# Summing fewer feature tiles of the second weight chunk in the startup of a two-layer mixer

## The chip, the core and the metric

The kernel runs on one core of a Trainium2 chip, as one program. The metric is device time in microseconds. The time before is 1073.24 us, the median of three runs (1071.56 to 1074.11). The profile is one execution, with a time of each instruction on the engines: PE multiplies matrices, DVE (VectorE) and ACT (ScalarE) work on tiles, SP issues the DMAs. "PE row" below means one matmul with 512 columns.

## The reference, cut

```python
# two layers; x (256 latent tokens x 2048), ctx (256 context tokens x 2048)
shift, scale, gate = split(silu(c) @ ada_w[l] + ada_b[l], 3)          # and the same for c_ctx
h  = rmsnorm(x, norm_g[l]) * (1 + scale) + shift                      # and hc from ctx
q, k, v, up, uf, g = split_proj(h @ w_in[l])
att = latent_attention(rope(rmsnorm(q)), [kc; rope(rmsnorm(k))], [vc; v])
mixed = concat(att, multiscale_pool(up), fourier_mix(uf))
x = x + gate * ((mixed * silu(g)) @ w_out[l])
...
return rmsnorm(x, final_norm_g)
```

What matters for this change is the first line of layer 0: the modulation needs 33.5 MB of `ada_w` before `h` is whole, and the products of `h` can begin feature tile by feature tile.

## The kernel before

Everything is kept transposed in 16 feature tiles of 128; latent and context tokens stand side by side (T = 512). Each product of float32 operands is made of three matmuls (high x high, high x low, low x high: `mm3`). `split` makes the two halves of a tile: ACT casts the high half (L138), DVE subtracts to get the low half (L139). Weights come as `raw` by DMA (L145) and are split to `whi` and `wlo`; each of the three names has three buffers. SP issues all loads in one queue, in an order that the scheduler sets; a load that waits for its buffer holds those behind it.

**The startup** of layer 0 (`startup`) makes `h0` and begins its products while the modulation loads.

- The statistics: the squares of x (ACT L862, DVE L860, sums L868), a product with ones (PE L871), then `rstd` (ACT L878, DVE L880). `load_x` brings x in four parts of 1 MB; three are asked for at once, the fourth behind the first piece of the modulation.
- The modulation comes in ten groups of 1 or 2 feature tiles (`GROUPS`: group 0 is tile 0, group 1 tile 1, group 2 tiles 2 and 3, ... group 7 tiles 12 and 13, group 8 tile 14, group 9 tile 15), each of four pieces (`a`, DMA L976, four buffers). `ada_part` multiplies a piece (PE L981). From group 5 on one piece of the four is done on DVE instead (`dvec`, L965).
- When a group's last piece is done, ACT copies the sums (`ev`, L1018), PE turns them (L1024), DVE reduces them (`red`, L1031) and adds the bias (L1038 to L1040), and `make_h` makes the group's tiles of `h`: DVE multiplies (L248, L255), ACT casts (L138), DVE subtracts (L139). The next group's sums use the same PSUM buffer and so wait for `red`.
- PE's order is written out by hand. `queue` puts a group's products on a list, ready one or two steps later, and `work(n)` issues n of them (L932) between the modulation's matmuls: 14 behind a piece of a group of two tiles, 7 behind one of a single tile, and 4 on either side of the turning.

The products of the startup are the first chunk of `w_in` (`accs`, 4 PSUM accumulators), the second chunk (`first`, 4 accumulators) and six tiles of the gate, three (`gfirst`) over the first `KG` = 4 feature tiles and three (`early`) over all. Eight PSUM buffers hold four large sums (`mm`) and four others (`sm`), so `accs` can only begin when `first` has been copied to `part` in SBUF. Before, `first` sums `KS` = 8 feature tiles; then chunk 0 is made up over tiles 0 to 7, and from tile 8 on it goes along with the modulation. Behind the startup `b_chunk` sums the second chunk's other tiles (L335 to L337), two tiles to a piece of weights, and adds `part`. `FILL` sets how many units of layer 1's modulation (DVE L188) each piece brings along.

`warm` issues matmuls of ones with ones, whose result is not used. `LAG_E` is the number of microseconds of queued products that PE puts between the evacuation of a chunk and the first use of it, for q the transposes at L525.

Of the kernel before, what the change touches and what calls it, by code (L numbers as in the profile page):

```python
# [12 lines left out]
F32 = mybir.dt.float32  # L13
# [7 lines left out]
P = 128  # L21
# [4 lines left out]
T = N + C  # L26
# [3 lines left out]

AHEAD = 400
ST = 4
KS = 8
ND = (0, 0, 0, 0, 0, 1, 1, 1, 1, 1)
KG = 4
NE = 3
# [10 lines left out]
LAG_S, LAG_T, LAG_E, LAG_Q = 4.3, 1.4, 5.6, 0.0  # L47
# [1 line left out]
LOW = -400  # L49
CHAIN = 200  # L50
PRE = 6
FILL = ((1.69, 1.5, 0.55, 1.43, 1.0), (0.04, 1.61, 0.01, 0.66, 0))
VB, VG, VF, VS, VC, VW = 0, 96, 128, 144, 152, 184


# [1 line left out]
def backbone(  # L57
# [24 lines left out]
    V, S, G, PE = nc.vector, nc.scalar, nc.gpsimd, nc.tensor  # L82

    const = ctx.enter_context(tc.tile_pool(name="const", bufs=1))
    hp = ctx.enter_context(tc.tile_pool(name="hp", bufs=1))
# [28 lines left out]
    def load_x(g, n):  # L114
        for j in range(0, 4, n):
            nc.sync.dma_start(xk[g][:, j : j + n], xT[:, 4 * g + j : 4 * g + j + n])
# [167 lines left out]
    side = Side()  # L284
# [86 lines left out]
    def f4(s, shape, dt=F32R):  # L371
        return late["f4"].tile(list(shape), dt, tag="f4", name=name(s))
# [145 lines left out]
    def q_prep(qraw, qT, rq):  # L518
        rq.append(head_rstd(qraw, 4, P ** -0.5))
        for tt, r in qraw:  # L520
            qo = rope_one(tt, r, 4, 0)
            yield 0.0, 3.0 if tt == 0 else 1.0
            tp = smt()
            for hh in range(4):
                PE.transpose(tp[:, hh * P : hh * P + P], qo[:, hh], idt)  # L525
            c = slice(tt * P, tt * P + P)
            split(tp.rearrange("p (h n) -> p h n", h=4), qT[0][:, :, c], qT[1][:, :, c])
            yield 0.43, 0.0
# [47 lines left out]
    def layer(l, h, xs, chunk0):  # L576
# [62 lines left out]
        for g in range(2):  # L639
            accs = b_chunk(l, 3 + g, h, ntt, FILL[l][2])  # L640
            qraw = evac_raw(accs)
            if l == 0:
                side.finish("a0")
                qT = pair8(4, (T,))
            else:
                qT = [a.rearrange("p a (b n) -> p (a b) n", b=2) for a in pair8(2, (2 * N,))]
            rq = []
            side.add(f"q{g}", q_prep(qraw, qT, rq), LAG_E, "k")
            for qt in range(ntt):
                side.add(f"a{g}", attention(g, qt, qT, rq, kT, vv, mixed, off), 0.0, f"q{g}")  # L650
        korder = list(range(8, 16)) + list(range(8))
# [177 lines left out]
            V.scalar_tensor_tensor(th, th, 1.0, g, op0=ALU.add, op1=ALU.mult)  # L829
        return th  # L830

    for g in range(3):
        load_x(g, 2)
    cq = [f4("cq", (P, 2, 512), F32) for _ in range(2)]
    h0 = H(T, "h")


    def startup():
        st = tc.tile_pool(name="st", bufs=ST)
        with st as st:  # L840
# [14 lines left out]
            def stats(g):  # L855
                q = [t2("sq") for _ in range(4)]
                for j in range(4):
                    x = xk[g][:, j]
                    if j == 3:
                        V.tensor_mul(q[j], x, x)  # L860
                    else:
                        i = S.activation(q[j], x, AF.Square)  # L862
                        if g == 0 and j == 0:
                            tc.add_manual_dep(
                                i.ins, root.ins.name, mybir.DependencyInfo(mybir.DependencyClass.NoSync, mybir.DependencyReason.DATA)
                            )
                    if j % 2:
                        V.tensor_add(q[j - 1], q[j - 1], q[j])  # L868
                pairs = [(o, c, j) for o, c in zip(ss, halves) for j in (0, 2)]
                for o, c, j in pairs if g == 3 else sorted(pairs, key=lambda e: e[2]):  # L870
                    PE.matmul(o[:, :N], ones, q[j][:, c], start=g == 0 and j == 0, stop=g == 3 and j == 2)  # L871
# [14 lines left out]
            accs = []  # L886
            part = ap_.tile([P, 4, T], F32, tag="A1", name="part")
            gpart = ap_.tile([P, 4, T], F32, tag="A0", name="gpart")
            backlog, jobs = [], []

            def rows(ready, ch, bs, k, i, b, s0, s1):
# [28 lines left out]
            def save(dst, src):  # L920
                for t, a in enumerate(src):
                    S.copy(dst[:, t], a)

            def work(n):
                while n > 0 and (backlog or jobs):
                    while jobs and len(backlog) < LOOK:
                        f, *a = jobs.pop(0)
                        f(*a)
                    if not backlog or backlog[0][0] > now[0]:
                        return  # L930
                    _, o, lt, r, s0, s1 = backlog.pop(0)
                    PE.matmul(o, lt, r, start=s0, stop=s1)  # L932
                    if s1 and o is first[-1]:
                        save(part, first)
                    if s1 and o is gfirst[-1]:
                        save(gpart, gfirst)
                    n -= 1
# [46 lines left out]

            def warm(n):
                for _ in range(n):
                    PE.matmul(first[3][:, :P], ones, ones, start=True, stop=True)

            with tc.manual_schedule(engines={mybir.EngineType.PE}):
                for g in range(3):  # L990
                    stats(g)
                for j, gs in enumerate(GROUPS):
                    a = smt()
                    w_ = 256 * gs
                    npc = 4 - ND[j]
                    raws = []
                    for kk in range(npc):
                        if j == 0 and kk == 1:
                            load_x(3, 1)
                        if j == 1 and kk == 3:  # L1000
                            late["store"]()
                        if kk == npc - 1 and j + 1 < len(GROUPS):
                            dvec(j + 1)
                        raws.append(piece(j, kk))
                        now[0] = 4 * j + kk + 4 - npc
                        if kk + 4 - npc == (PFK if j else 3):
                            queue(4 * j + 4 + (QK if j else Q0), k0, gs)
                        if j == 0 and kk == 2:
                            norm()
                        if j == 0 and kk == 3:  # L1010
                            nc.sync.dma_start(idt, ident)
                        ada_part(a, raws[kk], kk, kk == 0, kk == npc - 1, w_)
                        if j == 1 and kk < 2:
                            warm(3 - 2 * kk)
                        work(RATE * gs // 2)
                    with tc.high_priority(offset=CHAIN if j == 0 else 0):
                        ev = t2("ev")
                        S.copy(ev[:, :w_], a[:, :w_])  # L1018
                        if j:
                            work(4)  # L1020
                        else:
                            warm(3)
                        for q in range(2 * gs):
                            PE.transpose(a[:, q * P : q * P + P], ev[:, q * P : q * P + P], idt)  # L1024
                        if j:
                            work(4)
                        else:
                            store_cb(cvk, a[:32, 2 * P : 3 * P])
                            warm(2)
                        red = sp.tile([P, 2, gs, 2], F32, tag="red", name=name("red"))  # L1030
                        V.tensor_reduce(  # L1031
                            red.rearrange("p w k v -> p (w k) v"), a[:, :w_].rearrange("p (q g r) -> p q r g", g=4, r=32)[:, :, 0:2, :],
                            axis=AX.X, op=ALU.add,
                        )
                        dst = ab[0][:, :, k0 : k0 + gs]
                        bias = adab[:, : 2 * KT].rearrange("p (w k) -> p w k", w=2)[:, :, k0 : k0 + gs]
                        for e in range(ND[j]):
                            V.tensor_add(red, red, abq[:, e, :, k0 : k0 + gs])  # L1038
                        V.tensor_add(dst, red, bias.unsqueeze(3).to_broadcast([P, 2, gs, 2]))
                        V.tensor_mul(dst[:, 1], dst[:, 1], ng[:, k0 : k0 + gs].unsqueeze(2).to_broadcast([P, gs, 2]))  # L1040
                        for i in range(gs):
                            k = k0 + i
                            for vs in ((0,), (1,)) if k == 0 else ((0, 1),):
                                make_h(h0, k, xk[k // 4][:, k % 4], rstd, 0, vs)
                    k0 += gs
                now[0] = 10 ** 6
                work(LATE)
                pool_tables(0)
                fourier_loads(0)
                work(10 ** 6)  # L1050
                rope_tables(0)
# [131 lines left out]
```

## Time and profile before

| | |
|---|---|
| median of three runs | 1073.24 us |
| the profiled execution | 1073.19 us, span 1071.4 us |
| PE | 1047.4 us busy (98%) |
| weight loads of PE | 842.6 us (79%) |
| DVE | 842.3 us (79%) |
| ACT | 479.7 us (45%) |
| DMA | 233.63 MB, mean 218 GB/s |
| granted clock of PE | 0.998 |
| first product of the startup | 24.66 us |
| first matmul of the second chunk behind the startup | 170.45 us |

A busy time is the sum of an engine's instructions; PE's ends are modelled, so that a busy PE may still have small gaps. A row of the timeline gives the start, how long it took, the engine, the line, the operation, what is written and read, how many instructions were merged, and in brackets how long the engine had been idle and what ended it. A wait is listed as who waited for whom: microseconds in total, times, the longest.

### The profile page before, as it was taken

The page shows a single profiled execution, that of the slowest core. Times are in us where ns is not written, and L with a number is a line of the kernel's source. Part 1 is how long each engine was busy: PE and PEld are TensorE (multiplying, and loading weights), DVE is VectorE, ACT ScalarE, POOL GpSimd, SP SyncE. Part 2 cuts the span into 40 slices and gives each one's busy share as a digit, 9 for nine tenths or more (in the row PEclk, how much of TensorE's full clock was granted, in tenths as well). Part 3 has the DMA queues.
Part 4 walks back from the last instruction along what each step waited for, and adds up shares of the span by engine and source line. Part 5 has one row for each costly group of instructions (what it writes and reads, how often), then busy time and mean ns, then how long its engine had stood idle before and what let it go on. Part 6 is the DMA issues. An engine that isn't in the chain of part 4 may idle for free.

```text
span 1071.4 us, 14049 instructions
## 1 busy us (share of the span) xinstructions
PE 1047.4 (98%) x5100; PEld 842.6 (79%) x5100; DVE 842.3 (79%) x1553; ACT 479.7 (45%) x803; POOL 0.2 (0%) x4
## 2 busy tenths in 40 slices
PE   6899999999999999999999999999999999999996
PEld 4466677888787888888888888887888888888885
DVE  6358648998999779998989787489657889776565
ACT  5233225323323766632522223288326767447453
POOL 0000000000000000000000000000000000000000
PEclk9999999999999999999999999999999999999999
DMA  8999777566785244457776667445764565686563
GB/s 336 410 398 343 256 238 242 164 198 214 227 260 169 80 140 158 157 192 273 266 272 213 197 195 265 139 133 169 271 218 161 168 196 185 224 270 212 192 201 117
DMA packets 63797, 233.63 MB, mean 218 GB/s; under 512 B 7104, under 2 KB 8176, under 8 KB 60016
## 3 DMA queue, kind: packets, MB, share of 16 engines
q1 hardware_dynamic: 63152, 231.69, 63.8%
q10 hardware_dynamic: 576, 1.05, 0.3%
q8 instruction: 40, 0.66, 0.3%
q14 instruction: 29, 0.24, 0.1%
HBM read 230.58 MB, written 2.12 MB: 217 GB/s over the span
## 4 chain that ended last, share of the span: by engine, by line
PE 81%; DVE 7%; DMA 4%; ACT 3%; issue 3%; SPq 0%; DVEq 0%; ACTq 0%
PE mm L336 18%; PE mm L335 18%; PE mm L337 18%; PE mm L932 6%; PE mm L311 5%; PE sm L932 3%; DVE ajunk L188 2%; DMA a<-in_ada 2%; PE mm L312 2%; PE sm L336 2%; PE sm L337 2%; PE sm L335 2%; PE sm L981 2%; DVE wlo L139 2%; PE sm L562 1%
## 5 line engine op out<-in xcount | busy, mean ns | idle before, releaser
L138 ACT CAST whi<-raw 128x1024 fp32r<-128x1024 f32 (+1 forms) x216 | 219.9, 1019 | 333.0 <-PE mm L336 112.1
L139 DVE TENSOR_TENSOR wlo<-raw,whi 128x1024 fp32r<-128x1024 f32 (+1 forms) x216 | 255.3, 1182 | 103.7 <-ACT whi L138 102.6
L188 DVE SCALAR_TENSOR_TENSOR ajunk<-araw,cbt 128x1024 bf16<-128x1024 f32 x224 | 273.6, 1221 | 49.8 <-DMA araw<-in_adar 36.9
L335 PE MATMUL mm<-whi,h 128*128 128x512 f32 x416 | 167.6, 403 | 0.0
L336 PE MATMUL mm<-wlo,h 128*128 128x512 f32 x416 | 163.3, 393 | 0.0
L337 PE MATMUL mm<-whi,h 128*128 128x512 f32 x416 | 163.1, 392 | 0.0
L335 PE MATMUL mm<-m,whi 128*128 128x512 f32 (+1 forms) x272 | 102.6, 377 | 0.0
L336 PE MATMUL mm<-m,whi 128*128 128x512 f32 (+1 forms) x272 | 102.4, 377 | 0.0
L337 PE MATMUL mm<-m,wlo 128*128 128x512 f32 (+1 forms) x272 | 102.4, 377 | 0.0
L311 PE MATMUL mm<-h,whi 128*128 128x512 f32 x256 | 92.5, 400 | 0.0
L337 PEld LDWEIGHTS mm<-whi,h 128*128 128x128 f32 x416 | 78.1, 188 | 17.0 <-DVE h L139 0.3
L336 PEld LDWEIGHTS mm<-wlo,h 128*128 128x128 f32 x416 | 78.2, 188 | 16.2 <-issue 1.9
L335 PEld LDWEIGHTS mm<-whi,h 128*128 128x128 f32 x416 | 78.2, 188 | 16.1 <-issue 1.7
L335 PE MATMUL mm<-h,whi 128*128 128x512 f32 x196 | 77.7, 396 | 0.0
L337 PE MATMUL mm<-h,wlo 128*128 128x512 f32 x196 | 76.8, 392 | 0.0
L336 PE MATMUL mm<-h,whi 128*128 128x512 f32 x196 | 76.8, 392 | 0.0
L312 PE MATMUL mm<-h,wlo 128*128 128x256 f32 x256 | 72.4, 283 | 0.0
L932 PE MATMUL mm<-whi,h 128*128 128x512 f32 x192 | 63.8, 401 | 0.2 <-ACT h L138 0.2
L335 PEld LDWEIGHTS mm<-m,whi 128*128 128x128 f32 x272 | 51.2, 188 | 9.5
L337 PEld LDWEIGHTS mm<-m,wlo 128*128 128x128 f32 x272 | 51.2, 188 | 9.4
L336 PEld LDWEIGHTS mm<-m,whi 128*128 128x128 f32 x272 | 51.2, 188 | 9.2
L311 PEld LDWEIGHTS mm<-h,whi 128*128 128x128 f32 x256 | 48.1, 188 | 10.8
(229 smaller groups left out, 1639.1 us busy)
## 6 DMA issues: line engine op xcount, KB each, us to landing
araw<-in_adar SPq DMA_DIRECT2D x128, 512.0 KB, 4.0
raw<-in_wb SPq DMA_DIRECT2D x78, 512.0 KB, 3.6
raw<-in_wg SPq DMA_DIRECT2D x55, 512.0 KB, 4.3
a<-in_ada SPq DMA_DIRECT2D x24, 1024.0 KB, 9.1
raw<-in_wo SPq DMA_DIRECT2D x32, 512.0 KB, 4.3
raw<-in_wot SPq DMA_DIRECT2D x32, 512.0 KB, 3.9
a<-in_ada SPq DMA_DIRECT2D x16, 512.0 KB, 4.6
x<-in_xT SPq DMA_DIRECT2D x4, 1024.0 KB, 8.1
```

The lines of the kernel that those rows point to most:

```text
L138: i = S.copy(hi, src)
L139: V.tensor_sub(lo, src, hi.bitcast(F32))
L188: V.scalar_tensor_tensor(junk, raw, 1.0, cbt[:, v], op0=ALU.mult, op1=ALU.mult, accum_out=acc[:, u, h, v : v + 1])
L311: PE.matmul(a.rearrange("p (s n) -> p s n", s=2), hi[:, j - j0], h.both[k][:, :, :N], start=s0, stop=False)
L312: PE.matmul(a[:, :N], lo[:, j - j0], h.hi[k][:, :N], start=False, stop=s1)
L335: PE.matmul(o, ah, bh, start=start, stop=False)
L336: PE.matmul(o, ah, bl, start=False, stop=False)
L337: PE.matmul(o, al, bh, start=False, stop=stop)
L562: PE.transpose(tp[:, h * P : h * P + P], ps[h][:, i * P : i * P + P], idt)
L932: PE.matmul(o, lt, r, start=s0, stop=s1)
L981: PE.matmul(a[32 * i : 32 * i + 32, :w_], cs[:, 4 * kk + i], raw[:, i], start=first_, stop=last, tile_position=(0, 32 * i))
```

## The change

`KS` becomes 2: the second chunk is summed over feature tiles 0 and 1 alone in the startup. Its four accumulators are copied (L937 of the new program) to two buffers that `h0` needs for tiles 14 and 15 only (`lent`), since `part` lies where x of tiles 4 to 7 still is; behind group 4, when that x is used up, they are copied on to `part`. Chunk 0 is made up over tiles 0 and 1 and goes along with the modulation from tile 2 on. The second chunk's loop behind the startup has seven pieces of weights instead of four, with 1.0 units of filling each instead of 1.69. All of x is asked for ahead of the modulation, and the last statistics and `rstd` come ahead of the first `ada_part`. Ten matmuls of ones stand ahead of the statistics, and two behind each of the first three pieces of group 0; they write a gate accumulator instead of one of the second chunk. The preparation of q in layer 0 is set 1.5 later.

```diff
-KS = 8
+KS = 2
...
-FILL = ((1.69, 1.5, 0.55, 1.43, 1.0), (0.04, 1.61, 0.01, 0.66, 0))
+FILL = ((1.0, 1.5, 0.55, 1.43, 1.0), (0.04, 1.61, 0.01, 0.66, 0))
...
-            side.add(f"q{g}", q_prep(qraw, qT, rq), LAG_E, "k")
+            side.add(f"q{g}", q_prep(qraw, qT, rq), LAG_E + (1.5 if l == 0 else 0.0), "k")
...
-    for g in range(3):
-        load_x(g, 2)
+    for g in range(4):
+        load_x(g, 2 if g < 3 else 1)
     cq = [f4("cq", (P, 2, 512), F32) for _ in range(2)]
+    lent = [hp.tile([P, 2, T], F32, tag=f"h{k}", name=f"lent{k}") for k in (14, 15)]
...
+            spare = [lent[t // 2][:, t % 2] for t in range(4)]
...
                     if s1 and o is first[-1]:
-                        save(part, first)
+                        for t, a in enumerate(first):
+                            S.copy(spare[t], a)
...
-                    PE.matmul(first[3][:, :P], ones, ones, start=True, stop=True)
+                    PE.matmul(gfirst[0][:, :P], ones, ones, start=True, stop=True)
...
+                warm(10)
                 for g in range(3):
                     stats(g)
+                norm()
...
-                        if j == 0 and kk == 1:
-                            load_x(3, 1)
...
-                        if j == 0 and kk == 2:
-                            norm()
...
                         ada_part(a, raws[kk], kk, kk == 0, kk == npc - 1, w_)
+                        if j == 0 and kk < 3:
+                            warm(2)
...
                     k0 += gs
+                    if k0 == 8:
+                        save(part, spare)
```

What it does to the order is seen at three places. In the rows `h_3` is `h` of tile 0, `h_4` of tile 1 and so on up to `h_18`, tile 15; `mm` are accumulators of the two chunks, `sm` those of the gates or of the modulation, `a0` a piece of the modulation.

PE, group 2 (tiles 2 and 3), from its third piece to the turning, before:

```order
L981 MATMUL sm_73_360<-a0_76_387,cs_127 32x512 x4
L932 MATMUL sm_25_144<-h_4_109,wlo_68_322 128x512
L932 MATMUL sm_26_145<-h_4_109,whi_67_321 128x512 x2
L932 MATMUL sm_26_145<-h_4_109,wlo_68_322 128x512
L932 MATMUL sm_27_146<-h_4_109,whi_67_321 128x512 x2
L932 MATMUL sm_27_146<-h_4_109,wlo_68_322 128x512
L981 MATMUL sm_73_360<-a0_83_412,cs_127 32x512 x4
L1024 MATMUL sm_73_360<-idt_89,ev_84_418 128x128 x4
L981 MATMUL sm_88_440<-a0_89_441,cs_127 32x512 x4
L981 MATMUL sm_88_440<-a0_90_447,cs_127 32x512 x4
```

and now, from the fourth piece on (the seven rows before it are the first of chunk 0 over tile 0):

```order
L984 MATMUL sm_80_388<-a0_87_445,cs_133 32x512 x4
L934 MATMUL mm_71_345<-wlo_75_350,h_3_114 128x512
L934 MATMUL mm_71_345<-whi_74_349,h_3_114 128x512
...
L934 MATMUL mm_72_346<-wlo_75_350,h_4_115 128x512
L934 MATMUL mm_72_346<-whi_74_349,h_4_115 128x512
L1027 MATMUL sm_80_388<-idt_89,ev_91_471 128x128 x4
L984 MATMUL sm_95_496<-a0_96_497,cs_133 32x512 x4
L984 MATMUL sm_95_496<-a0_97_503,cs_133 32x512 x4
```

24 rows of chunk 0 over tiles 0 and 1 have moved in here, 7 ahead of the fourth piece and 17 between it and the turning.

PE at the turning of group 6 (tiles 10 and 11), before:

```order
L1024 MATMUL sm_155_832<-idt_89,ev_170_919 128x128 x4
L932 MATMUL mm_134_720<-whi_158_846,h_7_112 128x512
L932 MATMUL mm_134_720<-wlo_159_847,h_7_112 128x512
L932 MATMUL mm_134_720<-whi_158_846,h_7_112 128x512
L932 MATMUL mm_135_721<-whi_158_846,h_7_112 128x512
L981 MATMUL sm_174_950<-a0_175_951,cs_127 32x512 x4
L932 MATMUL mm_135_721<-wlo_159_847,h_7_112 128x512
```

and now:

```order
L1027 MATMUL sm_158_882<-idt_89,ev_173_969 128x128 x4
L984 MATMUL sm_177_992<-a0_178_993,cs_133 32x512 x4
L934 MATMUL mm_69_343<-whi_162_911,h_13_124 128x512
L934 MATMUL mm_69_343<-wlo_163_912,h_13_124 128x512
L934 MATMUL mm_69_343<-whi_162_911,h_13_124 128x512
```

The four rows behind the turning, and the rows behind the next piece, were chunk 0 over tile 4 (`h_7`); now none stand there, and those behind the piece read tile 10 (`h_13`), of the group just turned. Behind group 7's turning it is the same with tile 12, behind group 5's two rows are left ahead of the piece, and behind group 9's the nine gate rows of tile 14.

DVE at the turning of group 7 (tiles 12 and 13), before:

```order
L1031 TENSOR_REDUCE red_191_1051<-sm_174_950 128x8
L139 TENSOR_TENSOR wlo_190_1039<-raw_188_1036,whi_189_1038 128x1024
L1038 TENSOR_TENSOR red_191_1051<-red_191_1051,abq_84 128x8
L965 SCALAR_TENSOR_TENSOR junk_198_1097,abq_84<-a0_197_1095,cq_1_106 128x512
L1039 TENSOR_TENSOR ab0_96<-red_191_1051,vt_82 128x2x4
L965 SCALAR_TENSOR_TENSOR junk_199_1100,abq_84<-a0_197_1095,cq_1_106 128x512
L1040 TENSOR_TENSOR ab0_96<-ab0_96,vt_82 128x4
```

and now:

```order
L139 TENSOR_TENSOR wlo_199_1119<-raw_197_1116,whi_198_1118 128x512
L1034 TENSOR_REDUCE red_191_1079<-sm_177_992 128x8
L1041 TENSOR_TENSOR red_191_1079<-red_191_1079,abq_84 128x8
L1042 TENSOR_TENSOR ab0_96<-red_191_1079,vt_82 128x2x4
L968 SCALAR_TENSOR_TENSOR junk_204_1137,abq_84<-a0_203_1135,cq_1_110 128x512
L1043 TENSOR_TENSOR ab0_96<-ab0_96,vt_82 128x4
L968 SCALAR_TENSOR_TENSOR junk_205_1140,abq_84<-a0_203_1135,cq_1_110 128x512
```

The low half of a weight has moved from behind `red` to ahead of it; its high half (`whi_198`) takes the buffer of a gate weight that PE reads until the last row ahead of the turning. At the last turning, on ACT, the cast of the second chunk's next weight (`whi_269`, which takes the buffer of the gate weight of tile 14) stands ahead of the cast of tile 15.

## Prediction

> **What bounds the kernel now.** I read the page's busy times first, then the busy times in stretches of 10 us, then PE's own waits, then PE's rows in order of time. A "row" below is one 128x512 product of the startup (L932), TR is the transpose of a modulation (L1024), a "part" is the four matmuls of one modulation piece (L981, shown as x8).
>
> ```profile
> PE 1047.4 (98%) x5100; PEld 842.6 (79%) x5100; DVE 842.3 (79%) x1553; ACT 479.7 (45%) x803; POOL 0.2 (0%) x4
> ...
> 40.00:50.00 10.00, 7.78 (x45) 3.88 (x45) 6.80 (x14) 2.66 (x5) 0.00 (x0) 1.00 1.02 417
> 50.00:60.00 10.00, 10.00 (x51) 6.41 (x50) 2.16 (x3) 2.78 (x5) 0.00 (x0) 1.00 1.02 417
> ```
>
> ```profile
> PE sm L871 <- DVE sq L868: 7.7, 1, 7.7
> PE sm L981 <- DMA a<-in_ada: 3.0, 4, 1.2
> PE sm L525 <- DVE nt L235: 1.0, 1, 1.0
> PE sm L1024 <- ACT ev L1018: 0.7, 1, 0.7
> PE sm L981 <- DVE red L1031: 0.7, 2, 0.4
> PE sm L409 <- DVE th L829: 0.6, 1, 0.6
> ```
>
> PE is the bound: 24 us of the span are not PE's, 7.7 of them before the first statistic. From about 50 us on it hardly stops; what it waits for later is 0.6 us (L409) and 1.0 us (L525). All else that can be won lies before 47.60, where the modulation stream (DMA at 417 GB/s) paces PE:
>
> ```profile
> 24.66 0.50 PE L932 MATMUL mm<-whi,h 128*128 128x512 f32 x1 [0.23 <-ACT h L138]
> ...
> 35.37 0.50 PE L932 MATMUL mm<-whi,h 128*128 128x512 f32 x1
> ...
> 41.60 1.06 PE L981 MATMUL sm<-a,cs 128*32 128x512 f32 x8
> 43.37 0.66 PE L1024 MATMUL sm<-idt,ev 128*128 128x128 f32 x4 [0.71 <-ACT ev L1018]
> 44.38 1.06 PE L981 MATMUL sm<-a,cs 128*32 128x512 f32 x8 [0.35 <-DVE red L1031]
> 46.61 1.06 PE L981 MATMUL sm<-a,cs 128*32 128x512 f32 x8 [1.17 <-DMA a<-in_ada]
> 47.60 0.50 PE L932 MATMUL mm<-whi,h 128*128 128x512 f32 x1
> ```
>
> The listed gaps between 24.66 and 47.60 come to 3.7 us. The unit prices of a saturated PE:
>
> ```profile
> 66.61 1.06 PE L981 MATMUL sm<-a,cs 128*32 128x512 f32 x8
> 71.01 1.06 PE L981 MATMUL sm<-a,cs 128*32 128x512 f32 x8
> ...
> 128.54 0.64 PE L981 MATMUL sm<-a,cs 128*32 128x256 f32 x8
> 130.92 0.64 PE L981 MATMUL sm<-a,cs 128*32 128x256 f32 x8
> ...
> 145.72 0.38 PE L1024 MATMUL sm<-idt,ev 128*128 128x128 f32 x2
> 170.45 0.39 PE L335 MATMUL mm<-whi,h 128*128 128x512 f32 x1
> ```
>
> Behind the last TR stand 108 rows: (170.45 - 146.10) / 108 = 0.2255 us a row. 14 rows and a part take 4.40, so a part costs 1.24; 7 rows and a narrow part take 2.38, so 0.80.
>
> **The change, part by part.** Pure bookkeeping first: chunk 1 is now summed over 2 feature tiles in the startup instead of 8. That takes 72 rows (6 tiles x 12), 16.2 us, out of the startup and puts them as three more pieces into the chunk loop behind it, at the same price. It moves time and saves none. What counts is which idle time those rows covered.
>
> *Head.* Now the x loads stand together.
>
> ```profile
> 15.50 0.69 DVE L860 TENSOR_TENSOR sq<-x 128x512 f32<-128x512 f32 x1
> 16.29 0.69 DVE L868 TENSOR_TENSOR sq<-sq,sq 128x512 f32<-128x512 f32 x1
> ...
> 18.54 0.47 ACT L878 ACTIVATE rstd<-sm,epst 128x256 f32<-128x256 f32 x1 [3.02 <-PE sm L871]
> 19.04 3.37 DVE L880 RECIPROCAL rstd<-rstd 128x256 f32<-128x256 f32 x2 [2.05 <-ACT rstd L878]
> 22.32 0.11 DVE L1031 TENSOR_REDUCE red<-sm 128x4 f32<-128x16 f32 x1
> 23.16 0.68 DVE L139 TENSOR_TENSOR wlo<-raw,whi 128x512 fp32r<-128x512 f32 x1
> 23.91 0.33 SPq L145 DMA_DIRECT2D raw<-in_wgs  x1
> ...
> 24.00:26.00 2.00, 1.77 (x8) 1.10 (x8) 1.75 (x6) 1.35 (x3) 0.00 (x0) 1.00 0.60 170
> ```
>
> Without 0.5 MB of modulation ahead of the last x the last square comes about 1.3 us earlier, and without two parts between the statistics the reciprocals end at some 20.2 instead of 22.4. But the modulation needs the same 6 MB as before, so its part and its red come only about 0.4-1 us earlier; I put the first row at 23.3 (1.4 earlier) and the wlo that frees SP's next buffer at 21.9 (1.9 earlier). Behind that buffer SP now has a 0.5 MB weight load (tiles 0 and 1 of chunk 0) ahead of the modulation pieces: 1.2 us of transfer at 417 GB/s. It falls into the trough of 24-26 us (170 GB/s), so the pieces of group 2 land when they did. Its low part (1.2 us on DVE) now stands inside the chain to tile 1. Together the row of 35.37 stays where it is, 0.1 late at most. The ten fillers, of half a statistic's columns, take at most 0.53 us each (half of the 1.06 shown under the clock, below) and end before the first statistic could start, in the 7.7 us that PE waits anyway; six more of them between the parts of group 0 lie under the landing of its pieces, and would cost 2 us at the most were those there already. SP issues the first modulation piece behind four more x loads; with transfers in flight all that while, that costs nothing.
>
> *Group 2.* Before: 21 rows, two parts, TR, two parts in 12.23 us (35.37 to 47.60). Now 24 more rows stand there. 45 rows (10.15), two parts (2.48), TR to next part 1.01 (43.37 to 44.38), two parts back to back some 2.3: 15.9 us, against 12.23 + 24 x 0.2255 = 17.6. Gain 1.7; with the head **-1.5 us**. Ends: 0 (the transfers are late by the 0.5 MB) and -5.1 (all 3.7 us of gaps and the 1.4 of the first row).
>
> *Groups 3 to 5* have the same rows between the same parts as before: no change. The four copies to the lent buffers and the four back are ACT's, which is busy 27% in the stretches shown. The first four run while PE has the 9 gate rows of tile 1 and a part before it needs their accumulators' successors, the other four under the 18 rows ahead of group 4's TR: nothing, and 2.5 us (four at the 0.63 of a cast) if the casts of tiles 6 and 7 had to wait for them all.
>
> *Groups 6 to 9.* Here the 72 rows are missed. Before, 4 rows and a part and then rows of old tiles stand behind each TR; now, by the order, 2 rows and a part behind group 5's, a part alone behind those of groups 6 and 7, 9 rows behind the last, and then rows of the very tile that this TR has only begun. The chain from TR to that tile is in the trace, where rows hid it:
>
> ```profile
> 96.09 0.60 PE L1024 MATMUL sm<-idt,ev 128*128 128x128 f32 x4
> 96.73 0.19 DVE L1031 TENSOR_REDUCE red<-sm 128x8 f32<-128x32 f32 x1 [1.30 <-PE sm L1024]
> 97.56 1.39 DVE L255 TENSOR_SCALAR xn<-xn,ab 128x256 f32<-128x256 f32 x4
> 98.33 1.27 ACT L138 CAST h<-xn 128x512 fp32r<-128x512 f32 x2 [0.28 <-DVE xn L255]
> 99.99 1.29 DVE L139 TENSOR_TENSOR h<-xn,h 128x512 fp32r<-128x512 f32 x2
> ...
> 127.93 1.23 DVE L139 TENSOR_TENSOR wlo<-raw,whi 128x1024 fp32r<-128x1024 f32 x1
> ...
> 129.15 0.69 DVE L965 SCALAR_TENSOR_TENSOR junk<-a,cq 128x512 f32<-128x512 f32 x1
> ```
>
> The high half of the first tile is there 2.87 us after TR starts (98.33 + 0.63 - 96.09), the low half, which the third row needs, 0.7 later. Against that PE has: group 5: TR 0.36, 2 rows, a part, ready at 2.1: stall 0.85, and 0.25 before row 3: **1.1**. Group 6: no rows, and its part waits for red, as at 44.38; red itself is some 0.3 late, because the vector products of a piece (L965) end just then: first row at 3.3, row 3 0.2 late, instead of 1.6: **1.9**. Group 7: DVE now has ahead of red the low half of a weight whose high half waits for the last row before TR (0.62 + 0.68), and two L965 of 0.61 inside the chain: first row at 4.7, row 3 0.85 late, instead of 1.14: **4.4**. Group 8 has 18 rows and two parts: nothing. Group 9: on ACT the cast of chunk 1's next weight now stands ahead of the tile's high half, and it waits for the ninth row (2.45), with the tile's own cast queued behind it and PE waiting for that; then 1.0 for it and 0.62 for the tile, 4.3, and the low half behind a 1.2 us wlo: **2.7**.
>
> ```profile
> L138 ACT CAST whi<-raw 128x1024 fp32r<-128x1024 f32 (+1 forms) x216 | 219.9, 1019 | 333.0 <-PE mm L336 112.1
> ```
>
> Sum of the stalls **+10.1**. Lower end, with only the bare chain of 2.87 everywhere: 0.85 + 1.3 + 1.75 + 0.25 = 4.2. Upper end 12.3 (the clock, below).
>
> *Behind the startup.* The wait at L409 should go, because the gates' evacuation ends before PE comes to it; the wait of 1.0 at L525 should go, since q's preparation is set 1.5 us of work later. The smaller filling (1.0 x 7 units instead of 1.69 x 4) asks the same of DVE over more rows. **-1.5**, between -1.6 and +1 (a new wait of L525's size).
>
> **Sum** against the profiled execution's own 1073.19 (median of the runs 1073.24): 1073.19 - 1.5 + 10.1 - 1.5 = **1080.3 us**.
>
> **The clock.** The statistics show it cold and warm:
>
> ```profile
> 10.45 1.06 PE L871 MATMUL mm<-sq,ones 128*128 128x256 f32 x2
> ...
> 13.23 0.59 PE L871 MATMUL mm<-sq,ones 128*128 128x256 f32 x2
> ```
>
> For some 4.4 us from 7.7 on, these matmuls take twice as long. If a stall put PE back there, each time would cost half of such a stretch, 2.2 us; the longest gap before 170 us, 1.17 at 46.61, did not. The Trainium skill, "TensorE: Matmul & The Clock Gate", section "What's actually happening", says that the array falls back to half rate after an idle window of about 3.4 us. By that rule group 7's longest single gap (estimated 2.2 to 2.5 us) keeps the clock and the sum stays; no run here shows a gap of that size after the start.
>
> **Rivals.**
> 1. *Faster: the stalls are short and the head carries.* If the earlier wlo pulls the whole modulation stream forward, all 5.1 us are won, and with the bare chain at the late TRs: 1073.19 - 5.1 + 4.2 - 1.6 = 1070.7. It decides once the stalls stay under 6.7 us. For it: the trough at 24 us is real. Against it: the weight load put into that trough, and a DVE order that does stand in the chains. Chance 0.15.
> 2. *No change: bare chains only*, with my other terms: 1073.19 - 1.5 + 4.2 - 1.5 = 1074.4. For it speaks that DVE may reach red early. Chance 0.13.
> 3. *The clock falls back in the stalls:* 2.2 us more, 1082.5, and 1084.7 if it does so at group 9 too. Chance 0.10.
> 4. *The forecast,* 1080.3, between 1076 and 1084: 0.62.
>
> About 0.2% is what a measurement of this kernel can tell from no change: 2.1 us, so 1071.1 to 1075.4. Faster 0.15, same 0.13, slower 0.72. The range runs from 1071.5, which leaves out most of rival 1, to 1086, which takes in rival 3 and a bad end behind the startup.
>
> **What would show it.** In the changed trace PE's busy share stays near full from 35 us to the TR of tiles 8 and 9 (near 100 us), with no DMA wait at the second part of group 3. Then PE waits for ACT h and DVE h (L138, L139) four times, about 1, 2, 4 and 3 us, the third behind a wlo ahead of red. Chunk 1's first row stands near 163 us, where 154.2 would be even (170.45 - 16.2). Wrong would be: a first chunk-1 row at or before 155; a gap of several us before 47 us still there; waits of more than 2 us behind 170; a row spacing above 0.23 us after a stall.

## The result, and the profile after

The changed kernel takes 1087.05 us (median of four runs, 1086.74 to 1088.45) against 1073.28 before: a ratio of 1.0134, 95% interval 1.0119 to 1.0149. That is 13.8 us slower, where +7.1 was forecast, and 1 us above the upper end of the range. The profiled execution took 1086.77 us with a span of 1085.0, 13.6 above the span of 1071.4 before.

Busy time of PE, and then who PE waited for (microseconds, times, longest), after:

```profile
PE 1056.1 (97%) x5132; PEld 846.8 (78%) x5132; DVE 846.6 (78%) x1553; ACT 481.9 (44%) x807; POOL 0.2 (0%) x4
```

```profile
PE mm L934 <- ACT h L138: 5.6, 4, 2.4
...
PE sm L562 <- ACT p L550: 1.9, 2, 1.0
PE sm L984 <- DVE red L1034: 1.8, 3, 0.9
PE mm L934 <- DVE h L139: 1.1, 2, 0.6
...
PE sm L562 <- ACT p L545: 0.7, 2, 0.5
```

The first line did not exist before: four waits for the high halves of `h`, as forecast. L562 (the attention's transposes) is new at this size too; it had 0.4 us before. Of the 7.7 us before the first statistic 4.6 are now filled by matmuls of ones, which count as busy. The first statistic starts when it did (7.62 us, 7.73 before), but a row of two of the statistics' matmuls takes 0.59 us where it took 1.06.

To find where the 13.6 us arise, compare the same points of PE's rows. The timeline of after, with the transposes (L1027, "TR" as in the prediction) of groups 5 to 9 and the waits behind them:

```profile
25.99 0.48 PE L934 MATMUL mm<-whi,h 128*128 128x512 f32 x1
...
37.71 0.50 PE L934 MATMUL mm<-whi,h 128*128 128x512 f32 x1
...
53.53 0.50 PE L934 MATMUL mm<-whi,h 128*128 128x512 f32 x1
...
102.33 0.60 PE L1027 MATMUL sm<-idt,ev 128*128 128x128 f32 x4
105.24 0.50 PE L934 MATMUL mm<-whi,h 128*128 128x512 f32 x1 [0.84 <-ACT h L138]
...
117.64 0.60 PE L1027 MATMUL sm<-idt,ev 128*128 128x128 f32 x4
118.82 1.06 PE L984 MATMUL sm<-a,cs 128*32 128x512 f32 x8 [0.58 <-DVE red L1034]
120.84 0.50 PE L934 MATMUL mm<-whi,h 128*128 128x512 f32 x1 [0.96 <-ACT h L138]
...
133.24 0.60 PE L1027 MATMUL sm<-idt,ev 128*128 128x128 f32 x4
134.75 0.64 PE L984 MATMUL sm<-a,cs 128*32 128x256 f32 x8 [0.91 <-DVE red L1034]
137.74 0.50 PE L934 MATMUL mm<-whi,h 128*128 128x512 f32 x1 [2.36 <-ACT h L138]
...
147.45 0.38 PE L1027 MATMUL sm<-idt,ev 128*128 128x128 f32 x2
...
156.66 0.38 PE L1027 MATMUL sm<-idt,ev 128*128 128x128 f32 x2
...
160.58 0.50 PE L934 MATMUL mm<-whi,h 128*128 128x512 f32 x1 [1.47 <-ACT h L138]
...
166.37 0.39 PE L335 MATMUL mm<-whi,h 128*128 128x512 f32 x1
```

The same transposes before, between 96.09 and 145.72:

```profile
111.59 0.38 PE L1024 MATMUL sm<-idt,ev 128*128 128x128 f32 x2
127.07 0.38 PE L1024 MATMUL sm<-idt,ev 128*128 128x128 f32 x2
136.51 0.38 PE L1024 MATMUL sm<-idt,ev 128*128 128x128 f32 x2
```

Rows were moved between the stretches, so each is compared at equal work: 0.2255 us is added or taken off for each row more or less. Group 5's transpose stood at 96.09; with the 24 rows that now come ahead of it, 101.5 would be even.

| stretch | before | rows | even | after | difference |
|---|---|---|---|---|---|
| start to TR of group 5 | 96.09 | +24 | 101.50 | 102.33 | +0.8 |
| group 5's TR to group 6's | 15.50 | -6 | 14.15 | 15.31 | +1.2 |
| group 6's to 7's | 15.48 | -8 | 13.68 | 15.60 | +1.9 |
| group 7's to 8's | 9.44 | -4 | 8.54 | 14.21 | +5.7 |
| group 8's to 9's | 9.21 | 0 | 9.21 | 9.21 | 0 |
| group 9's to chunk 1 | 24.73 | -78 | 7.14 | 9.71 | +2.6 |
| behind it, to the end | 900.95 | +72 | 917.19 | 918.63 | +1.4 |

Of the 13.6 us, 11.4 lie behind the last transposes. Six rows fewer behind a transpose saved 1.35 us of work and brought a stall of 1.2.

Group 7's 5.7 us are more than its waits (0.91 + 2.36 and 0.47 for a low half). Its stretch in slices of 2 us shows why; the third figure from the end is the granted clock:

```profile
134.00:136.00 2.00, 0.64 (x8) 0.16 (x8) 1.93 (x8) 0.00 (x0) 0.00 (x0) 1.00 0.08 33
136.00:138.00 2.00, 0.26 (x1) 0.26 (x2) 2.00 (x7) 0.90 (x2) 0.00 (x0) 1.00 0.72 242
138.00:140.00 2.00, 1.53 (x6) 0.91 (x6) 2.00 (x5) 0.34 (x1) 0.00 (x0) 0.88 0.87 313
140.00:142.00 2.00, 2.00 (x12) 0.54 (x10) 0.71 (x3) 0.00 (x0) 0.00 (x0) 0.50 0.55 164
142.00:144.00 2.00, 2.00 (x7) 1.51 (x7) 0.00 (x0) 0.00 (x0) 0.00 (x0) 0.76 0.86 205
```

PE did 0.90 us of work between 134 and 138 us, and a moment later its clock was at half for (0.12 + 0.50 + 0.24) x 2 / 0.5 = 3.4 us, while rows were there to do.

### The profile page after: what moved, and what is told of

It reads as the page before. It is cut to its first block, busy times and chain, and to the rows that moved or that the text cites. A ratio compares the mean times of both kernels' runs of the same rounds, so it can differ in the third digit from the quotient of the medians.

```text
span 1085.0 us, 14119 instructions
## 1 busy us (share of the span) xinstructions
PE 1056.1 (97%) x5132; PEld 846.8 (78%) x5132; DVE 846.6 (78%) x1553; ACT 481.9 (44%) x807; POOL 0.2 (0%) x4
## 4 chain that ended last, share of the span: by engine, by line
PE 86%; DVE 4%; DMA 4%; ACT 3%; issue 2%; SPq 1%; ACTq 0%; DVEq 0%
PE mm L336 21%; PE mm L337 21%; PE mm L335 21%; PE mm L311 4%; PE mm L934 4%; PE sm L934 3%; PE mm L312 2%; DMA araw<-in_adar 2%; PE sm L984 2%; PE sm L336 2%; PE sm L337 2%; PE sm L335 2%; PE sm L562 1%; DVE wlo L139 1%; ACT whi L138 1%
## 5 line engine op out<-in xcount | busy, mean ns | idle before, releaser
L138 ACT CAST whi<-raw 128x1024 fp32r<-128x1024 f32 (+3 forms) x216 | 219.9, 1019 | 341.1 <-PE mm L337 120.4
L139 DVE TENSOR_TENSOR wlo<-raw,whi 128x1024 fp32r<-128x1024 f32 (+3 forms) x216 | 255.0, 1181 | 107.9 <-ACT whi L138 106.5
L335 PE MATMUL mm<-whi,h 128*128 128x512 f32 x440 | 177.5, 403 | 0.0
L337 PE MATMUL mm<-whi,h 128*128 128x512 f32 x440 | 172.3, 392 | 0.0
L336 PE MATMUL mm<-wlo,h 128*128 128x512 f32 x440 | 172.3, 392 | 0.0
L336 PE MATMUL mm<-m,whi 128*128 128x512 f32 (+1 forms) x272 | 102.4, 377 | 0.0
L337 PEld LDWEIGHTS mm<-whi,h 128*128 128x128 f32 x440 | 82.6, 188 | 17.7 <-DVE h L139 0.3
L336 PEld LDWEIGHTS mm<-wlo,h 128*128 128x128 f32 x440 | 82.7, 188 | 17.2 <-issue 1.9
L335 PEld LDWEIGHTS mm<-whi,h 128*128 128x128 f32 x440 | 82.8, 188 | 17.0 <-issue 1.9
L336 PE MATMUL mm<-h,whi 128*128 128x512 f32 x196 | 76.7, 391 | 0.0
L336 PEld LDWEIGHTS mm<-m,whi 128*128 128x128 f32 x272 | 51.2, 188 | 9.3
L311 PEld LDWEIGHTS mm<-h,whi 128*128 128x128 f32 x256 | 48.1, 188 | 10.8
L934 PE MATMUL mm<-whi,h 128*128 128x512 f32 x144 | 49.2, 411 | 6.8 <-ACT h L138 5.6
```

The costliest lines, as they stand in the source:

```text
L138: i = S.copy(hi, src)
L139: V.tensor_sub(lo, src, hi.bitcast(F32))
L311: PE.matmul(a.rearrange("p (s n) -> p s n", s=2), hi[:, j - j0], h.both[k][:, :, :N], start=s0, stop=False)
L335: PE.matmul(o, ah, bh, start=start, stop=False)
L336: PE.matmul(o, ah, bl, start=False, stop=False)
L337: PE.matmul(o, al, bh, start=False, stop=stop)
```

## The experiments

Two theories stood against each other at first: A, the loss is the late transposes without rows behind them; B, the new head (x first, fillers, statistics ahead of the parts) carries it. C (q's later preparation costs time) and D (held modulation buffers) came up on the way. All ratios are to the kernel before, run beside them on the same chip (1073.36 us beside `head_only`, `tiles_only`, `clock_kept` and `chain_first`, 1072.46 beside `ks4`, `ks4_old_head`, `q_lag0` and `no_part_fill`, 1072.2 beside `k4_lag`, `k4_fill169`, `parts_early` and `best_try`). A span or a row is that of the one profiled execution.

**`head_only`: the new head alone.**

```diff
-KS = 2
+KS = 8            # with the old copies, filling 1.69, no lent buffers
```

> The changed kernel with chunk 1 summed over 8 feature tiles in the startup again (its old copies and filling 1.69, no lent buffers); x whole ahead, the fillers and q's preparation 1.5 later stay. Theory A (the loss is the late transposes without cover): only the head's delay is left, the first row near 26.0 and tile 1's first row near 37.7 as in the changed kernel (24.66 and 35.37 before); the late stalls are gone; 2.3 us of delay less at most 1.6 won behind the startup: 1073.5 to 1076. Theory B (the new head carries the loss): 1080 or more.

1077.38 us, ratio 1.0044 (1.0026 to 1.0063): above A's 1076 and below B's 1080. No wait for `h` is left, and the spacing of the late transposes is the old one. Tile 1's first row is at 36.28, 0.9 later than before, and chunk 1's at 171.36, 0.9 later too. But the span is 3.4 longer: 2.5 us are lost behind the startup, where there was nothing but q's preparation. The new head does not carry the loss, and theory B falls; the 2.5 are theory C's.

**`tiles_only`: the four accumulators alone.**

```diff
-KS = 8            # in the kernel before
+KS = 2            # with lent buffers, copies and filling 1.0; all else old
```

> The kernel before with only the four accumulators lent at the second feature tile (2 tiles instead of 8, lent buffers, copies back at tile 8, filling 1.0). x in its old order, no fillers ahead of the statistics or between the parts of group 0, q's preparation as before. Theory A: first row 24.7, tile 1 at 35.4, then 1.7 won in group 2 and the stalls of 1, 2, 4 and 3 us behind the transposes of groups 5, 6, 7 and 9, with a stretch at half clock behind group 7's: 1073.2 - 1.7 + 10 + 1.4, so 1081 to 1085. Theory B: at most 1077.

1087.34 us, ratio 1.0137 (1.0111 to 1.0163): as slow as the whole change, by itself. The forecast of its first 50 us was wrong, though: tile 1 stands at 39.20 and not at 35.4. SP's queue tells why, before and here (start and time of an issue, then the line and what is loaded):

```profile
23.91 0.33 SPq L145 DMA_DIRECT2D raw<-in_wgs  x1
24.34 0.38 SPq L160 DMA_DIRECT2D cd<-crow  x1
24.77 2.96 SPq L976 DMA_DIRECT2D a<-in_ada  x4
```

```profile
24.03 0.33 SPq L145 DMA_DIRECT2D raw<-in_wgs  x1
25.09 0.33 SPq L145 DMA_DIRECT2D raw<-in_wb  x1
25.47 0.84 SPq L160 DMA_DIRECT2D cd<-crow  x1
26.41 1.81 SPq L979 DMA_DIRECT2D a<-in_ada  x4
```

Two tiles bring one weight load more (`raw<-in_wb`), chunk 0's, ahead of the modulation. It waits for its buffer until 25.09, everything behind it waits with it, and the pieces of the modulation are asked for 1.6 us later, with 0.5 MB ahead of them. Behind PE's waits for them (1.43 and 1.32 us) the clock also fell to half, from 37 to 41 us. In the runs with four or eight tiles tile 1's first row comes 9.6 to 11.6 us after those pieces are asked for, with two tiles 11.3 to 13.7.

**`ks4`: the changed kernel with four tiles.**

```diff
-KS = 2
+KS = 4
```

> The changed kernel with four feature tiles of chunk 1 in the startup instead of two; the lent buffers, filling, x order, fillers and q's later preparation stay. By its order PE has the same rows behind every transpose as the kernel before has, up to the last, behind which stand 63 rows instead of 111 (33 with two tiles). Theory A (the loss in the startup is the late transposes without rows behind them): the spacing of the late transposes is the old one (15.5, 15.5, 9.4, 9.2), no wait for ACT h or DVE h there, chunk 1's first row 13.9 us behind the last transpose and near 160.5 (159.6 would be even); with what q's later preparation costs, 2.5 us by the first runs: 1076 to 1078. Theory B (lending the buffers or the earlier copies cost by themselves): stalls of some us remain between 80 and 150 us, 1081 or more.

1074.89 us, ratio 1.0024 (1.0013 to 1.0035): 12 us less than with two tiles. The waits for `h` are gone. From the last transpose to chunk 1:

```profile
148.31 0.38 PE L1027 MATMUL sm<-idt,ev 128*128 128x128 f32 x2
...
162.15 0.39 PE L335 MATMUL mm<-whi,h 128*128 128x512 f32 x1
```

13.84 us for 60 rows (63 with chunk 1's first three), against 24.73 for 108 before: 48 rows less are 10.8 us less, and nothing is lost. The lent buffers, the extra copies and 48 of the 72 rows moved out cost nothing there. Of the 11.7 us between this span and that of the changed kernel, 11.4 lie behind the late transposes; the head (1.8 worse here) and the part behind the startup (2.1 better here) nearly cancel. The last 24 of those rows, 5.4 us of work, were the ones that covered four chains. This is the run that settles theory A. (Chunk 1's row was expected at 160.5; a stretch at half clock at 47 to 51 us, behind DMA waits of 1.04 and 1.33, made it 162.15.)

**`ks4_old_head`: four tiles without the other parts.**

```diff
-KS = 8            # in the kernel before
+KS = 4            # with lent buffers, copies and filling 1.0; all else old
```

> The kernel before with four tiles of chunk 1 in the startup, lent buffers and filling 1.0; old order of x, no new fillers, q's preparation as before. Theory A: the first 50 us as before (tile 1 at 35.4, tile 2 at 47.6), old spacing of the late transposes, chunk 1's first row near 159.6, and behind it the filling of 1.0 wins what it won with two tiles, 1.5: 1071.8; without that win 1073.3. Theory B: 1077 or more.

1071.76 us, ratio 0.9995 (0.9985 to 1.0004): no difference that can be measured. Against `tiles_only`, two tiles instead of four cost 1.4% here, 15 us.

**`clock_kept`: fillers under group 7's wait.**

```diff
+if j == 8 and kk == 0:
+    warm_to(a[:, :P], 10)      # ten 128x128 products ahead of group 8's first part
```

> The changed kernel with ten filler products (128x128, about 0.2 us each) ahead of group 8's first part, under the wait behind group 7's transpose; they write the accumulator that this part then overwrites. If the clock fell because PE stood still behind that transpose: first row of group 7's tiles still near 137.7, no slice under 1.0 of granted clock between 138 and 146 us, and 1.4 us less: 1085.6. If the slow rows have another cause: the same 1087 with the slow rows still there. If the fillers stand in the way of the part or of the rows: 1087.5 or more.

1088.1 us, ratio 1.0138 (1.0122 to 1.0155). On the spot it did what was expected: the clock stays, and from group 7's transpose (135.40) to group 8's (148.10) it takes 12.70 us instead of 14.21.

```profile
136.91 2.50 PE L990 MATMUL sm<-ones 128*128 128x128 f32 x20 [0.92 <-DVE red L1040]
139.34 0.64 PE L984 MATMUL sm<-a,cs 128*32 128x256 f32 x8
```

```profile
138.00:140.00 2.00, 2.00 (x22) 1.46 (x20) 2.00 (x7) 0.73 (x2) 0.00 (x0) 1.00 0.88 334
140.00:142.00 2.00, 1.52 (x6) 0.96 (x7) 2.00 (x5) 0.51 (x1) 0.00 (x0) 1.00 0.46 139
142.00:144.00 2.00, 2.00 (x15) 1.08 (x14) 0.89 (x3) 0.00 (x0) 0.00 (x0) 1.00 0.63 211
```

So the slow stretch cost 1.5 us and came from PE's standing still. The total did not fall: in this execution the modulation came late (a DMA wait of 2.65), with a half-clock stretch at 32 to 35 us, and tile 1 began at 39.66; the clock fell once more at 404 to 408 us. Whether the fillers have a part in that stays open.

**`chain_first`: group 7's chain without the products in it.**

```diff
+held.append((j, e, gs, k0, raw))
+if j not in HOLD:                     # HOLD = (8,)
+    products()
 ...
+products(late["low"])                 # behind make_h, after its last low half
```

> The changed kernel with VectorE's products for group 8 held until behind group 7's own low halves, so that no product of 0.68 us stands between group 7's red and its tiles; nothing else on PE changes. If two products inside the chain cost what the trace shows: group 7's first row at 136.4 instead of 137.7, the gap 1.0 instead of 2.36, and with so short a gap no fallen clock, 1.4 + 1.4 less: about 1084.2 (1085.7 if the clock falls all the same). If PE waits there for something else: 1087, the first row where it was. Group 8's sum could wait for the held products: then a new wait ahead of tile 14.

1089.19 us, ratio 1.0147 (1.013 to 1.0163). VectorE's rows behind group 7's transpose, in the changed kernel and here:

```profile
133.90 0.69 DVE L139 TENSOR_TENSOR wlo<-raw,whi 128x512 fp32r<-128x512 f32 x1 [2.70 <-ACT whi L138]
134.51 0.18 DVE L1034 TENSOR_REDUCE red<-sm 128x8 f32<-128x32 f32 x1
...
135.70 0.68 DVE L968 SCALAR_TENSOR_TENSOR junk<-a,cq 128x512 f32<-128x512 f32 x1
...
136.31 1.38 DVE L255 TENSOR_SCALAR xn<-xn,ab 128x256 f32<-128x256 f32 x4
```

```profile
137.18 0.18 DVE L1048 TENSOR_REDUCE red<-sm 128x8 f32<-128x32 f32 x1
...
138.00 1.38 DVE L256 TENSOR_SCALAR xn<-xn,ab 128x256 f32<-128x256 f32 x4
```

From red to the products of x it takes 0.82 instead of 1.80, PE's gap is 1.38 instead of 2.36, the clock stays, and group 7's transpose (135.91) to group 8's (147.12) takes 11.21 us instead of 14.21: 3.0 won on the spot, a little more than the 2.8 expected. The rest gave it back: the modulation came late here too (a DMA wait of 2.35, a half-clock stretch at 32 to 36 us, tile 1 at 40.18), and the clock fell at 162 to 166 us and at 404 to 408 us instead. The chain's price is confirmed, the gain over the whole is not.

**`q_lag0`: the changed kernel, q's preparation at its old time.**

```diff
-side.add(f"q{g}", q_prep(qraw, qT, rq), LAG_E + (1.5 if l == 0 else 0.0), "k")
+side.add(f"q{g}", q_prep(qraw, qT, rq), LAG_E, "k")
```

> The changed kernel with q's preparation at its old delay, nothing else. Theory C (the later preparation costs time in the attention: the kernel with the new head and eight tiles lost 2.5 us behind 171 us, the one with two tiles and the old delay won 1.5 there): startup as in the changed kernel, waits at L562 back to some 0.5 from 2.6, 2.5 to 2.9 us less, about 1084.3. If the later preparation is harmless or helps, as was forecast: 1087 to 1088.5, with a wait of 1.0 at L525 back.

1085.91 us, ratio 1.0120 (1.0105 to 1.0135), 1.5 us less than the changed kernel's ratio gives; the two intervals overlap. Behind chunk 1's first row (167.0) 917.0 us are left instead of 918.63. L562 fell only to 1.6, not to 0.5.

**`k4_lag`: q's later preparation alone, on `ks4_old_head`.**

```diff
-side.add(f"q{g}", q_prep(qraw, qT, rq), LAG_E, "k")
+side.add(f"q{g}", q_prep(qraw, qT, rq), LAG_E + (1.5 if l == 0 else 0.0), "k")
```

> The kernel before with four tiles in the startup, lent buffers and filling 1.0 (1071.8 in its run), and q's preparation 1.5 units later; no other part of the change. Theory C (the later preparation costs time in the attention): startup as without it, waits at L562 up from 0.7 to some 2 us, 1.5 to 2.5 us slower than without it: 1073.3 to 1074.3. If it is harmless: 1071.8, and the waits at L562 in the other runs had another cause.

1073.75 us, ratio 1.0019 (1.0011 to 1.0028), against 0.9995 (0.9985 to 1.0004) without it: 0.24%, 2.6 us, and the intervals are apart. Theory C stands. PE's waits at L562, with and without:

```profile
PE sm L562 <- ACT p L550: 1.5, 2, 0.8
...
PE sm L336 <- DVE ptl L139: 0.8, 2, 0.5
```

```profile
PE sm L336 <- DVE ptl L139: 1.8, 2, 1.3
...
PE sm L562 <- ACT p L550: 0.7, 1, 0.7
```

The two spans behind chunk 1's first row differ by 1.0 us only, so the trace shows the direction and not the whole of the 2.6. The waits do not show the cause: what PE waits longer at L562 it waits less at L336, which is the attention's too. Matmul by matmul from chunk 1's first row, the two traces stay within 0.4 us of each other up to 388 us, and at 475 us the one with the delay is 1.3 behind (2.55 for the changed kernel against `q_lag0`, at 481 us). In between stand the first transposes of the attention. So the place is known, and what costs the time there stays open.

The other traces agree on the sign. From chunk 1's first row on and at equal work, the five kernels with the old delay and fewer tiles are 0.2 to 1.6 us shorter than the kernel before; the eight with the later one lie between 0.6 shorter and 3.1 longer.

**`k4_fill169`: the old filling, on `ks4_old_head`.**

```diff
-FILL = ((1.0, 1.5, 0.55, 1.43, 1.0), ...
+FILL = ((1.69, 1.5, 0.55, 1.43, 1.0), ...
```

> The kernel before with four tiles in the startup and lent buffers, but the filling of chunk 1 at its old 1.69; no other part of the change. If the smaller filling is what removes the waits of 0.6 at L409 and 1.0 at L525: both are back and the time is 1073.3, as before. If it is without effect, or the longer chunk loop alone removes them: 1071.8. If too much work is set on VectorE and ScalarE in the longer loop: 1074 or more, with new waits behind 160 us.

1072.57 us, ratio 1.0004 (0.9995 to 1.0012). That overlaps with 0.9995: no effect that can be told. The wait at L409 is not back with it, the one at L525 only with 0.5 us.

**`no_part_fill`: no fillers between the parts of group 0.**

```diff
-if j == 0 and kk < 3:
-    warm(2)
```

> The changed kernel without the six fillers between the four parts of group 0 (the ten ahead of the statistics stay). If the pieces of group 0 have landed when PE comes to their parts: parts 0.80 apart instead of 1.21, group 0's transpose at 21.1 instead of 22.3, first row 24.8 instead of 26.0, tile 1 near 36.5 instead of 37.7, 1.2 us less: 1085.8. If the fillers lie under the landing, as was forecast: waits for DMA ahead of those parts and the same 1087. If they keep the clock up: slow rows ahead of 35 us, and up to 1089.

1087.68 us, ratio 1.0138 (1.0121 to 1.0155). Three of the four pieces had landed, so the fillers did lie on the path: the parts stand together, and group 0's transpose is at 20.66 instead of 22.34. But the rows of PE that now wait do so for a transfer:

```profile
17.18 1.50 PE L984 MATMUL sm<-a,cs 128*32 128x256 f32 x24
...
24.91 0.64 PE L984 MATMUL sm<-a,cs 128*32 128x256 f32 x8 [1.60 <-DMA a<-in_ada]
...
25.72 0.48 PE L934 MATMUL mm<-whi,h 128*128 128x512 f32 x1
```

The first row gains 0.27 us of the 1.7, tile 1 (36.31) gains 1.4, and over all runs no gain is left.

**`parts_early`: the last statistic back between the parts.**

```diff
-norm()
 for j, gs in enumerate(GROUPS):
 ...
+        if j == 0 and kk == 2:
+            norm()
```

> The changed kernel with the last statistic back between the second and the third part of group 0, x still loaded whole ahead of the modulation, fillers as they are. Theory D (the parts that were moved behind the last statistic hold the four modulation buffers longer, and SP can issue group 1's pieces only when they come free): SP's first piece of group 1 at 16.5 instead of 18.07, tile 1's first row near 36.2 instead of 37.7, 1.5 us less: 1085.5. If the transfers themselves are the limit: the pieces are issued earlier and land when they did, tile 1 at 37.7 and 1087.

1088.87 us, ratio 1.0161 (1.0147 to 1.0174). SP's first piece of group 1 goes out at 16.76 instead of 18.07, as theory D says, but `rstd` and group 0's transpose (22.76) come later, and with them the low half that frees SP's next weight buffer: 25.25 instead of 24.01. The four pieces are asked for at 27.20, and tile 1 begins at 40.54, behind a DMA wait of 2.77 and a half-clock stretch at 34 to 38 us. The weight buffers hold the modulation, not its own buffers: theory D falls.

**`best_try`: the parts that did no harm, together.**

```diff
-KS = 2
+KS = 4            # no warm(2) between the parts, norm() at kk == 2, q at LAG_E
```

> Four tiles of chunk 1 in the startup with lent buffers and filling 1.0, x loaded whole first, ten fillers ahead of the statistics, the last statistic between the second and third part of group 0, no fillers between those parts, q's preparation at its old delay. By theory A no stall behind the late transposes. If the head then wins what it was meant to win by theory D, tile 1's first row at 34.9 or before and 1070.5 to 1071.3, below the kernel before; if the transfers are the limit, 1071.8 to 1073.

1071.75 us, ratio 0.9999 (0.999 to 1.0007). Tile 1 begins at 34.79, 0.6 earlier than before, and that is all; it beats the changed kernel by 1.3% and equals the kernel before.

## Why the prediction was right and wrong

**Right: the stalls.** Term by term, forecast and measured (from the table above): group 5's transpose 1.1 and 1.2, group 6's 1.9 and 1.9, group 8's 0 and 0, group 9's 2.7 and 2.6. Group 7's was 4.4, measured 5.7 with the fallen clock, which `clock_kept` prices at 1.5; without it 4.2. The sum of 10.1 is 11.4 with the clock and 9.9 without. Counting the rows that stand behind each transpose and setting the chain of the trace against them was enough, and `ks4` shows that those rows were the cause. Group 9's order was the forecast one as well: on ACT the cast of chunk 1's next weight started at 158.97, and tile 15's behind it at 159.92.

**Wrong: the clock (rival 3, put at 0.10).** It came true at group 7, at 1.5 us in this trace and at 0.9 to 2.2 in the four others that have the same waits, where 2.2 was forecast. The forecast took the Trainium skill's rule as a point in favour of the clock. "TensorE: Matmul & The Clock Gate", section "What's actually happening", speaks of an idle window of about 3.4 us, running freely. Slow stretches of 3.4 us or twice that (below), and their coming and going from run to run, agree with such a window. The idle time does not: the longest single gap here was 2.36 us, with a part of 0.64 us ahead of it, and the clock fell; the measurement decides.

**Wrong: the head (-1.5, measured +0.8).** Group 2 did gain: 15.82 us from 37.71 to 53.53, with 15.9 forecast. The failing steps lie ahead of it. First, "six more of them ... lie under the landing of its pieces" and so were put at 0: with them group 0's transpose is at 22.34, without them at 20.66. Second, the `wlo` that frees SP's buffer was put at 21.9, 1.9 earlier than its end at 23.84 before; it ran from 23.25 to 23.93 in the changed kernel, and from 21.57 to 22.25 once those fillers were out. Third, the 0.5 MB weight load "falls into the trough": the trough is filled (323 GB/s at 24 to 26 us, 170 before), but the load waits for a buffer of its own, so that the modulation behind it was asked for at 26.38 instead of 24.77. In `no_part_fill` it was asked for at 24.69, and tile 1 (36.31) still came 0.9 later than before. The first row, put at 23.3, came at 25.99, and tile 1's row, "0.1 late at most", was 2.3 late.

**Wrong: behind the startup (-1.5, measured +1.4).** The failing step is "the wait of 1.0 at L525 should go, since q's preparation is set 1.5 us of work later". The waits at L409 and L525 did shrink, but not for that reason: in `ks4_old_head`, without that part, the wait at L525 is gone as well, and the one at L409 is 0.2, while a new one of 1.8 stands at L336. In `tiles_only`, again without it, this part of the kernel is 1.5 shorter at equal work, as forecast. The later preparation itself costs 2.6 us (`k4_lag`), where the forecast had set it down as a gain of 1.0. It named "a new wait of L525's size" as the upper end. The loss is larger, and it arises at the first transposes of the attention (L562), whose work is queued behind q; the forecast's list of later waits had left out the 0.4 us that L562 had before. Which engine or wait makes the loss there stays open.

So most of the loss was forecast at the right place and size. The missing 6.5 us are the head (2.3), the part behind the startup (2.9) and, for the rest (1.3), the clock. Head and tail were both set down as small gains, read from waits that "should go", without a price for what the same edit makes late.

## What to carry to other kernels

Rows that sit behind a serial chain are cover, and the last ones are worth more than their own time: 48 rows could leave the startup for nothing, and 24 more cost 12 to 15 us, some 11 of them behind the late transposes. Before work is moved out, count for each chain what is left beside it, and stop at the last number that still covers it. A wait that "should go" is worth nothing in a forecast until it is named what then comes last there.

## What the hardware showed that was not expected

PE's clock fell to half behind one long wait or several close together, and not in every execution. The longest wait ahead of such a fall was between 0.90 us (at 402 us in `clock_kept`, with 0.22 and 0.45 behind it) and 2.77 us (`parts_early`). A single wait of that size need not do it: behind 1.17 us at 46.61 in the kernel before and 1.26 us at L336 in `ks4_old_head` the clock stayed. Behind group 9's waits of 1.47 and 0.61 us it stayed in the changed kernel and fell in `tiles_only` and `chain_first`.

Behind group 7's waits of 0.91 and 2.36 us it fell in all five traces that have them, but not for the same time: for 3.4 us in the changed kernel and `tiles_only`, and for twice that in `q_lag0`, `parts_early` and `no_part_fill`, here the last:

```profile
136.00:138.00 2.00, 1.43 (x3) 0.72 (x4) 2.00 (x6) 1.14 (x2) 0.00 (x0) 0.50 0.96 342
138.00:140.00 2.00, 2.00 (x5) 1.28 (x5) 1.54 (x4) 0.00 (x0) 0.00 (x0) 0.50 0.55 205
140.00:142.00 2.00, 2.00 (x11) 0.89 (x11) 0.00 (x0) 0.00 (x0) 0.00 (x0) 0.50 0.68 248
142.00:144.00 2.00, 2.00 (x15) 1.21 (x13) 0.00 (x0) 0.00 (x0) 0.00 (x0) 0.83 0.71 258
```

That is (3 x 0.50 + 0.17) x 2 / 0.5 = 6.7 us, and from group 7's transpose to group 8's it takes 14.88 us, where the other four need 13.62 to 14.87 and `clock_kept`, with the clock kept up, 12.70. So waits of 1 to 2 us, close together, can cost more than their sum, and one profile does not tell how much more. Over all executions the kernels with two tiles ran with a mean clock of 0.989 to 0.995, against 0.998 in the profile of before.
